# Second mixer of a two-layer hybrid diffusion block: elementwise work moved off GpSimd, small matrix products cut into array tiles, router logits in column tiles

## The chip, the cores and the metric

One Trainium2 chip, one NeuronCore of it. The metric is the device time of one execution in microseconds (us), the median of three runs. The engines are TensorE (PE; its weight loads are listed apart as PEld), VectorE (DVE), ScalarE (ACT), GpSimd (POOL) and SyncE (SP), which issues most DMAs. PE, DVE, ACT and POOL each work through their own instructions in order.

## The reference, cut to what matters

Two layers follow each other on 512 latent and 256 context tokens of width 1024. Each layer is a mixer and then a mixture of 16 experts in which every expert chooses its tokens. Only the second layer's mixer is touched by the change, with the router of both layers.

```
# second mixer: a recurrence in both directions (8 heads of 64), and attention in a window
p = p + mu * (0.5 * (p[t-1] + p[t+1]) - p)                      # centred shift of the projections
w = -softplus(-(w0[d] + tanh(wl) @ w2[d])) - 0.5;  a = sigmoid(a0[d] + al @ a2[d])      # d = 0, 1
dec, keys = exp(-exp(w)), k * (1 + (a - 1) * k_a);  kk = normalised(k * k_k)
S = S * dec + (S @ -kk) (x) (kk * a) + v (x) keys;  y = S @ r    # per token, per direction
win = softmax([scores in a window of 128 | scores on the context | sink]) @ values
# router
aff = softmax(h @ w_router)           # 16 experts; each takes its 64 (context: 32) best tokens
```

## The kernel before, in words

All products are in float32 (two PE passes, so a product counts as two instructions in the trace) except those written as `F32R` or `H16`. A tile framework orders the instructions of the mixers by priority from the program order and inserts the waits; the order on an engine is fixed at build time.

`mixer0`, then `moe` for layer 0, then `mixer1`, then `moe` for layer 1. Within `mixer1`:

- **Front** (`front`, `shifted`, `features`). 33 blocks of 128 columns of the input projection are made by `project` (products `pj`, weights split into two parts by `weights`: `wraw` to `wblk`). `shifted` adds the neighbours in time: ScalarE copies the product to `pd`, GpSimd adds two shifted views into `sh`, and VectorE combines. `features` makes decay, rate and keys for two 128-token tiles of one pair of heads: the low-rank products `lw` with `w2` and `a2`, which are padded with zeros so that each direction uses the whole array, then a chain of elementwise work in the tiles called `lo` (`sig` and `aa`), a scan (`cl`) and the factors A and B, stored in DRAM (`fa`, `fb`).
- **prep**, 24 times (two directions, two groups of heads, six tiles of 128 tokens; two of the six are context tiles). It loads A and B as AR and BK, makes the 64x64 Gram products `gr` of both chunks, masks them (GA, GR), and inverts the triangular matrix by doubling (tiles Th, X, Z, Q; products `pf`, `px`, `pz`, `pc`), with one correction step in float32 (`pe`, tiles Tt and X32).
- **chain**, 24 times two chunks: the recurrence over chunks, with products `an`, `pu`, `pn` and the states `N`; latent tiles also give the output `y`.
- **win_attend**, after the front: 32 head-and-block steps with scores `sw`, softmax weights P (`Pw`), transposes `ptw` to `PTw`, values `po`, and a transpose `orw` of the result to `winT`.
- **finish** and **projected**: group norm of the recurrence's output and the output projection (`op`).

Front, prep, chain and window are generators stepped in turn, so their instructions interleave on every engine. When the last tile's recurrence is done, SBUF is freed for a ring of six 2 MB slots (`open_ring(6)`), two more slots follow when the router's memory is free, and SP then streams 302 MB of expert weights (`we`, `wd`) for layer 1 through them. `route_tile` normalises a tile, transposes it to `ht` and forms the logits `lg`; in layer 0 its stages are stepped between the halves of the output projection (`op`, L774).

The Gram products, and the products of a 64-row state, use zeros in the tile of A to keep two heads apart:

```
for h in range(2):
    for p in range(2):
        nc.sync.dma_start(AR[hd[h], p, :, h], self.fa[d, tt, hd[h], 2 * u + p])   # other half of AR stays zero
...
nc.tensor.matmul(pb[:, 2 * w * c:2 * w * c + 2 * w], BK[:, p, c], AR[:, p, c, :, 0:w // 64], start=True, stop=True)
```

Of the kernel before, what the change touches and what calls it, by code (L numbers as in the profile page):

```python
# [99 lines left out]
class Kern:  # L100
# [690 lines left out]
    def mixer1(self):  # L791
# [69 lines left out]
        def weights():  # L861

            while len(cut) < 2 and (queue or order):
# [8 lines left out]
                (nc.vector if len(order) % 2 else nc.gpsimd).tensor_tensor(w[:, 1], raw, w[:, 0].bitcast(F32), OP.subtract)  # L872
# [9 lines left out]
        nc.gpsimd.tensor_copy(id16[:, 0:128], self.ident)  # L882
        nc.gpsimd.tensor_copy(id16[:, 128:192], id64)
# [46 lines left out]
        def shifted(blk, a, out):  # L930

            n = a[0].shape[2]
            for pb in project(a, 1024 // n):
                yield
            pd = fo.tile([128, NLAT + 2], F32, name="pd")
            nc.gpsimd.memset(pd[:, 0:n + 2:n + 1], 0.0)
            nc.scalar.activation(pd[:, 1:n + 1], pb, AF.Copy)
            s = fo.tile([128, NLAT], F32, name="sh")
            nc.gpsimd.tensor_tensor(s[:, :n], pd[:, 0:n], pd[:, 2:n + 2], OP.add)
            if n < NLAT or blk % 2:  # L940
                nc.vector.tensor_scalar(out, pb, om[:, blk:blk + 1], None, OP.mult)
            else:
                nc.scalar.activation(out, pb, AF.Copy, scale=om[:, blk:blk + 1])
            nc.vector.scalar_tensor_tensor(out, s[:, :n], hm[:, blk:blk + 1], out, OP.mult, OP.add)
# [6 lines left out]
        def features(p, t0, kp, rp, vp, low):  # L951
# [61 lines left out]
            for d in dirs:  # L1013
                nc.gpsimd.tensor_tensor(aa[d], aa[d], kp, OP.mult)
# [164 lines left out]
        def win_attend(ww, kd, V, q, band):  # L1179
# [4 lines left out]
            Ps, PTs, os, sums = {}, {}, {}, {}  # L1184
# [5 lines left out]
            def scores(n):  # L1190
# [23 lines left out]
                nc.vector.reciprocal(m[:, 2:3], m[:, 2:3])  # L1214

            def turn(n):
# [3 lines left out]
                pt = PTs[n] = ww.tile([128, nk, 128], F32, name="PTw", tag="PTw", bufs=3)  # L1220
# [8 lines left out]
            def values(n):  # L1229
                i, b, a = heads[n]  # L1230
                j0, nk = keys(b)
                pt = PTs.pop(n)
# [5 lines left out]
                if a == 0:  # L1238
                    os[n // 2] = ww.tile([128, 128], F32, name="ow", tag="ow", bufs=2)
                nc.scalar.activation(os[n // 2][:, 64 * a:64 * a + 64], po[:, 0:64], AF.Copy, scale=sums.pop(n)[:, 2:3])  # L1240

            def rows(m):
                i, b, _ = heads[2 * m]
                pr = self.bank("orw")
# [907 lines left out]
```

## Time and profile before

| | us |
|---|---|
| three runs | 2968.59, 2965.43, 2972.07 (median 2968.59) |
| the profiled execution: its time | 2972.21 |
| its span, first to last instruction | 2970.4 |
| mean granted TensorE clock | 0.954 of full speed |
| busy: PE, DVE, ACT, POOL | 2660.2, 1322.9, 742.6, 471.4 |

The span divides into layer 0's mixer (to about 560 us), layer 0's experts (to about 1446), the second mixer (1446 to 2205) and layer 1's experts (from 2258, with the first weights from 2204 on). A granted clock of 1.00 is 2.4 GHz, 0.50 is 1.2 GHz; a mean between them over a stretch is a mix of the two. Busy shares hide stages with different limits, so the stages are read one by one.

### The profile page before, as it was taken

The numbers are of one execution on the slowest core, as the hardware profiler recorded it, in microseconds if no ns is written. First come the engines' busy times: TensorE is split into PE (matmuls) and PEld (weight loads), VectorE is DVE, ScalarE is ACT, GpSimd is POOL, SyncE is SP. The second block draws the span as 40 slices with busy tenths as digits, with TensorE's granted clock in tenths as the row PEclk, the third lists the DMA queues.
The fourth block names the chain that finished last, engine by engine and source line by source line (L and its number), as shares of the span: only waits on it lengthen the run. The fifth ranks groups of instructions, "written<-read, shape, count | busy, mean of one in ns | idle before, by whom it ended". The sixth has DMA issues, their size and how long they took to land.

```text
span 2970.4 us, 47837 instructions
## 1 busy us (share of the span) xinstructions
PE 2660.2 (90%) x19606; PEld 1535.4 (52%) x19606; DVE 1322.9 (45%) x3546; ACT 742.6 (25%) x1718; POOL 471.4 (16%) x591
## 2 busy tenths in 40 slices
PE   7999999799999999999878878799987987888886
PEld 4787776544444444444466656587653332333322
DVE  4323665444234334322475777677654332223312
ACT  3212444211111111101354544366321111101111
POOL 2332003200000000000283553411210000000000
PEclk9999999799999999999987988899987999999999
DMA  9765001488988988988642233310349999999997
GB/s 329 244 246 175 27 12 57 172 333 353 371 356 355 371 345 367 365 355 355 216 126 73 86 108 120 111 32 28 118 184 377 426 427 427 427 426 427 426 427 314
DMA packets 176587, 779.47 MB, mean 262 GB/s; under 512 B 24327, under 2 KB 110768, under 8 KB 133488
## 3 DMA queue, kind: packets, MB, share of 16 engines
q1 hardware_dynamic: 169200, 752.31, 64.5%
q0 software_dynamic: 3872, 12.52, 1.2%
q10 hardware_dynamic: 3296, 11.58, 1.0%
q8 instruction: 155, 2.54, 0.4%
q14 instruction: 64, 0.52, 0.1%
HBM read 745.68 MB, written 30.67 MB: 261 GB/s over the span
## 4 chain that ended last, share of the span: by engine, by line
PE 64%; DMA 19%; DVE 9%; POOL 3%; ACT 3%; issue 2%; SPq 0%; POOLq 0%; ACTq 0%; DVEq 0%
PE gu L1924 13%; PE ydn L1992 9%; DMA wd<-in_moe_w_down_dram 8%; DMA we<-in_moe_w_gate_up_dram 8%; PE guc L1937 6%; PE ydc L1996 3%; PE pj L926 3%; PE pj L411 2%; PE pj L412 2%; PE pj L413 2%; PE op L774 2%; PE op L1556 2%; PE adap L231 2%; PE sc L593 1%; PE scp L1816 1%
## 5 line engine op out<-in xcount | busy, mean ns | idle before, releaser
L1924 PE MATMUL gu<-we,xs 128*64 128x512 f32 x3072 | 687.9, 597 | 83.5 <-DMA we<-in_moe_w_gate_up_dram 83.4
L1924 PEld LDWEIGHTS gu<-we,xs 128*64 128x64 f32 x3072 | 216.7, 137 | 520.5 <-issue 408.5
L1992 PE MATMUL ydn<-wd,uT 128*64 128x512 f32 x1536 | 351.8, 600 | 14.3 <-DMA wd<-in_moe_w_down_dram 13.7
L1930 DVE TENSOR_TENSOR sg<-gu,sg 64x512 f32<-64x512 f32 x96 | 66.5, 693 | 458.4 <-ACT sg L1929 457.8
L1929 ACT ACTIVATE sg<-gu 64x512 f32<-64x512 f32 x96 | 56.8, 592 | 846.3 <-PE gu L1924 846.3
L1776 POOL DMA_INDIRECT xg<-xnd,idx x22 | 20.9, 952 | 1246.6 <-DVE gate L1781 1186.0
L1992 PEld LDWEIGHTS ydn<-wd,uT 128*64 128x64 f32 x1536 | 107.9, 137 | 205.3 <-issue 187.0
L1937 PE MATMUL guc<-we,xs 128*32 128x256 f32 x3072 | 172.6, 380 | 0.0
L926 PE MATMUL pj<-aL,wblk 128*128 128x512 f32 x504 | 158.1, 448 | 0.0
L1937 PEld LDWEIGHTS guc<-we,xs 128*32 128x32 f32 x3072 | 96.4, 110 | 68.4 <-issue 7.5
L411 PE MATMUL pj<-ah,wblk 128*128 128x384 f32 (+1 forms) x320 | 109.5, 343 | 1.4 <-ACT ah L380 1.4
L926 PEld LDWEIGHTS pj<-aL,wblk 128*128 128x128 f32 x504 | 99.0, 210 | 18.4
L412 PE MATMUL pj<-al,wblk 128*128 128x384 f32 (+1 forms) x320 | 107.9, 338 | 0.0
L413 PE MATMUL pj<-ah,wblk 128*128 128x384 f32 (+1 forms) x320 | 107.4, 336 | 0.0
L1819 DVE TENSOR_TENSOR x<-scp,x 128x512 f32<-128x512 f32 x144 | 92.3, 684 | 30.3 <-PE scp L1817 29.4
L1996 PE MATMUL ydc<-wd,uTc 128*32 128x256 f32 x1536 | 90.6, 380 | 1.4 <-DMA wd<-in_moe_w_down_dram 1.4
L1906 DVE COPY uTc<-utc 128x128 f32<-128x128 f32 x48 | 14.0, 291 | 172.6 <-PE utc L1904 172.1
L2046 DVE TENSOR_TENSOR yp<-ydn,gbc 64x512 f32<-64x512 f32 x64 | 44.1, 689 | 103.8 <-PE ydn L1992 103.3
L1796 DVE TENSOR_SCALAR xs<-xst,gm,modT 128x128 f32<-128x128 f32 (+1 forms) x88 | 34.8, 397 | 118.9 <-PE xst L1788 115.7
L1900 ACT ACTIVATE uT<-utp 128x256 f32<-128x256 f32 x96 | 36.0, 375 | 159.4 <-PE utp L1899 158.6
L1382 DVE STREAM_TRANSPOSE Zbd<-X 64x256 f16<-64x256 f16 x144 | 62.7, 436 | 24.2 <-ACT X L1376 21.8
L1996 PEld LDWEIGHTS ydc<-wd,uTc 128*32 128x32 f32 x1536 | 47.6, 110 | 43.9 <-issue 15.2
(421 smaller groups left out, 4630.4 us busy)
## 6 DMA issues: line engine op xcount, KB each, us to landing
we<-in_moe_w_gate_up_dram SPq DMA_DIRECT2D x192, 2048.0 KB, 13.5
wd<-in_moe_w_down_dram SPq DMA_DIRECT2D x95, 2048.0 KB, 11.8
adaw<-in_ada_w_dram SPq DMA_DIRECT2D x48, 1024.0 KB, 6.5
wraw<-in_od_w_in_dram SPq DMA_DIRECT2D x33, 512.0 KB, 4.2
wraw<-in_ev_w_in_dram SPq DMA_DIRECT2D x19, 512.0 KB, 6.8
fb<-B SPq DMA_DIRECT2D x24, 256.0 KB, 2.5
BK<-fb SPq DMA_DIRECT2D x24, 256.0 KB, 3.0
xnd<-xn ACTq DMA_DIRECT2D x10, 512.0 KB, 4.7
```

The lines of the kernel that those rows point to most:

```text
L231: nc.tensor.matmul(pb[32 * j:32 * j + 32], self.spad[:, k, :], w[:, 512 * j:512 * j + 512], start=k == 0, stop=k == 7, tile_position=(0, 3 ...
L411: nc.tensor.matmul(pb[:m, :384], w[:, 0, k, 0:m], ah[k][:, t], start=k == 0, stop=False)
L412: nc.tensor.matmul(pb[:m, :384], w[:, 0, k, 0:m], al[k][:, t], start=False, stop=False)
L413: nc.tensor.matmul(pb[:m, :384], w[:, 1, k, 0:m], ah[k][:, t], start=False, stop=k == 7)
L926: nc.tensor.matmul(pb[:, :n], w[:, i, k], a[j][:, k], start=k + i + j == 0, stop=k == 7 and i == 1)
L1382: nc.vector.transpose(Zd[h], X[hd[h]])
L1819: nc.vector.tensor_tensor(xs, pb, xs, OP.add)
L1924: nc.tensor.matmul(gu[64 * j:64 * j + 64, :], g.xs[:, k, 64 * a:64 * a + 64], ws[j][k], start=k == 0, stop=k == 7, tile_position=(0, 64 * j))
L1930: nc.vector.tensor_tensor(sg, gu[64:128], sg, OP.mult)
L1937: nc.tensor.matmul(guc[32 * j:32 * j + 32, 0:256], q.xs[:, k, 32 * a4:32 * a4 + 32], ws[j // 2][k][:, 256 * (j % 2):256 * (j % 2) + 256], ...
L1992: nc.tensor.matmul(y[64 * h:64 * h + 64, :], uT[:, f], wt[i][:, 512 * h:512 * h + 512], start=f == 0, stop=f == 11, tile_position=(0, 64 * h))
L1996: nc.tensor.matmul(yc[32 * j:32 * j + 32, 0:256], uTc[:, f], wt[i][:, 256 * j:256 * j + 256], start=f == 0, stop=f == 11, tile_position=(0 ...
```

## The change

- **GpSimd's work.** The second half of the weight split goes to VectorE always. `shifted` has no copy, no neighbour sum on GpSimd: ScalarE scales the product out of PSUM, and VectorE adds the two neighbours straight from PSUM with two shifted instructions. In `features` three elementwise steps go to ScalarE (`sig`, the scaling of `aa`) and VectorE (`aa` times `kp`). In `prep`, Tt becomes a ScalarE copy (the identity that was subtracted comes back as a product with minus the identity), the masking of Z goes to VectorE, and Zc is copied from PSUM by ScalarE. In `chain` the decay is applied after the sum, by VectorE, and the product `n0s` is gone.
- **Tiles of the array.** `w2` and `a2` hold both directions without zeros and their products use 64 rows each; AR has half the size, no zeros, and is loaded by one DMA (two for context tiles) in the place of four; `gr`, `an` and the first product of `y` use 64-row tiles. `pe` is three kinds of products into one accumulation: the identity once over 256 columns, minus the identity times X over 256 columns, and Tt times X for the four chunks.
- **Window.** ScalarE scales P by the reciprocal sum before the transposes; `values` handles two heads at once, with V as the stationary operand and 128 columns of `PTw` moving, so the transpose `orw` and the per-head copies are gone. `values` comes one step later; `Pw` and `PTw` have four buffers for three.
- **Router.** The logits are formed as four partial sums in column tiles of 32, copied by ScalarE to `ls`, and summed by one product with `rsum`. The router's weights `wr` live in the router's own pool and are loaded when it opens.

```diff
-                (nc.vector if len(order) % 2 else nc.gpsimd).tensor_tensor(w[:, 1], raw, w[:, 0].bitcast(F32), OP.subtract)
+                nc.vector.tensor_tensor(w[:, 1], raw, w[:, 0].bitcast(F32), OP.subtract)
...
-            pd = fo.tile([128, NLAT + 2], F32, name="pd")
-            nc.gpsimd.memset(pd[:, 0:n + 2:n + 1], 0.0)
-            nc.scalar.activation(pd[:, 1:n + 1], pb, AF.Copy)
-            s = fo.tile([128, NLAT], F32, name="sh")
-            nc.gpsimd.tensor_tensor(s[:, :n], pd[:, 0:n], pd[:, 2:n + 2], OP.add)
...
-            nc.vector.scalar_tensor_tensor(out, s[:, :n], hm[:, blk:blk + 1], out, OP.mult, OP.add)
+            nc.scalar.activation(out, pb, AF.Copy, scale=om[:, blk:blk + 1])
+
+            for o, s in ((1, 0), (0, 1)):
+                o = out[:, o:n - 1 + o]
+                nc.vector.scalar_tensor_tensor(o, pb[:, s:n - 1 + s], hm[:, blk:blk + 1], o, OP.mult, OP.add)
...
-                    nc.tensor.matmul(pb[d][:, 0:256], wt[:, d, 128 * p:128 * p + 128], src, start=True, stop=True)
+                    nc.tensor.matmul(pb[d][:, 0:256], wt[64 * d:64 * d + 64, 128 * p:128 * p + 128],
+                                     src[64 * d:64 * d + 64], start=True, stop=True, tile_position=(64 * d, 0))
...
-                        nc.gpsimd.tensor_scalar(sig[d], sig[d], 0.5, 0.5, OP.mult, OP.add)
+                        nc.scalar.activation(sig[d], sig[d], AF.Identity, bias=half, scale=0.5)
...
-                nc.gpsimd.tensor_scalar(aa[d], aa[d], hka[:, p:p + 1], oka[:, p:p + 1], OP.mult, OP.add)
+                nc.scalar.activation(aa[d], aa[d], AF.Identity, bias=oka[:, p:p + 1], scale=hka[:, p:p + 1])
...
-                nc.gpsimd.tensor_tensor(aa[d], aa[d], kp, OP.mult)
+                nc.vector.tensor_tensor(aa[d], aa[d], kp, OP.mult)
...
+                nc.scalar.activation(P, P, AF.Copy, scale=m[:, 2:3])
...
-                    nc.tensor.matmul(po[:, 0:64], pt[:, c], V[:, c if c < 2 else j0 + c, 64 * kv:64 * kv + 64],
-                                     start=c == 0, stop=c == nk - 1)
...
+                    for a in range(2):
+                        nc.tensor.matmul(po[64 * a:64 * a + 64, 0:128],
+                                         V[:, c if c < 2 else j0 + c, 64 * kv:64 * kv + 64], pt[a][:, c],
+                                         start=c == 0, stop=c == nk - 1, tile_position=(0, 64 * a))
...
-                nc.tensor.transpose(pr[:, 0:128], os.pop(m), self.ident)
...
+            for g in range(4):
+                for h in range(2):
+                    nc.tensor.matmul(pb[h][:, w * g:w * g + w], BK[hd[h], g // 2, g % 2],
+                                     AR[hd[h], g // 2, g % 2, 0:w // 64], start=True, stop=True,
+                                     tile_position=(64 * h, 0))
...
-                nc.gpsimd.tensor_tensor(Ttd[h], GA[0:64, :, h], id64[0:64, None, :].to_broadcast([64, 4, 64]),
-                                        OP.subtract)
+                nc.scalar.activation(Ttd[h], GA[0:64, :, h], AF.Copy)
...
-                nc.gpsimd.tensor_tensor(Zd[h], Thd[h], lev(0, 1 - d)[hd[h]], OP.mult)
+                nc.vector.tensor_tensor(Zd[h], Thd[h], lev(0, 1 - d)[hd[h]], OP.mult)
...
+            nc.tensor.matmul(v3(pf), id16[:, 0:128], id16[:, None, 128:192].to_broadcast([128, 4, 64]), start=True,
+                             stop=False)
+            nc.tensor.matmul(v3(pf), minus, X, start=False, stop=False)
             for c in range(4):
-                o = pf[:, 64 * c:64 * c + 64]
-                nc.tensor.matmul(o, Tt[:, c], X[:, c], start=True, stop=False)
-                nc.tensor.matmul(o, id16[:, 0:128], id16[:, 128:192], start=False, stop=True)
+                nc.tensor.matmul(pf[:, 64 * c:64 * c + 64], Tt[:, c], X[:, c], start=False, stop=c == 3)
...
-                nc.gpsimd.tensor_tensor(n0s, n0, dec[:, :, None].to_broadcast([128, 2, 64]), OP.mult)
...
-                        nc.tensor.matmul(pa[hd[h], 64 * p:64 * p + 64], AR[:, p, c, h, 0], n0[:, p],
-                                         start=True, stop=True, tile_position=(0, 64 * h))
+                        nc.tensor.matmul(pa[hd[h], 64 * p:64 * p + 64], AR[hd[h], p, c, 0], n0[hd[h], p],
+                                         start=True, stop=True, tile_position=(64 * h, 64 * h))
...
-                for p in range(2):
-                    nc.vector.scalar_tensor_tensor(N1[:, p], a2_(pn)[:, p], dec[:, p:p + 1], n0s[:, p], OP.mult, OP.add)
+                nc.vector.tensor_tensor(N1, a2_(pn), n0, OP.add)
+                nc.vector.tensor_tensor(N1, N1, dec[:, :, None].to_broadcast([128, 2, 64]), OP.mult)
...
+        for i in range(2):
+            for j in range(4):
+                nc.tensor.matmul(lp[32 * j:32 * j + 32, 0:128], self.rwr[:, 4 * i + j], ht[:, 4 * i + j], start=i == 0,
+                                 stop=i == 1, tile_position=(0, 32 * j))
+        ls = self.rtw.tile([128, 128], F32, name="ls")
+        nc.scalar.activation(ls, lp[:, 0:128], AF.Copy)
...
-        for k in range(8):
-            nc.tensor.matmul(lg[:, 0:16], ht[:, k], self.rwr[:, k], start=k == 0, stop=k == 7)
+        nc.tensor.matmul(lg[:, 0:16], ls, self.rsum, start=True, stop=True)
```

On GpSimd, in the front while the first latent feature blocks are made, these rows stand before (`sh`, `pd`: neighbour sum; `lo`: decay and rate; `Ttbd`, `Zbd`: two tiles of prep; `n0s`: decayed state; `ssq`, `nrm`: norm of the key):

```order
L1428 TENSOR_TENSOR n0s<-N_13101,PL 128x128
L1341 TENSOR_TENSOR Ttbd_12035<-GA,m_11064 64x4x64 x2
L1357 TENSOR_TENSOR Zbd_12031<-Thbd_12029,lev_11053 64x4x64 x2
L939 TENSOR_TENSOR sh<-pd 128x512
L1009 TENSOR_SCALAR lo<-lo,hka,oka 128x256
L936 MEMSET pd 128x2
L1014 TENSOR_TENSOR lo<-lo,ko 128x256
L1009 TENSOR_SCALAR lo<-lo,hka,oka 128x256
L1014 TENSOR_TENSOR lo<-lo,ko 128x256
```

and in the changed kernel GpSimd has, in the whole of that stage, only these kinds:

```order
L1131 TENSOR_SCALAR sgl<-sgl 128x512
L1019 COPY PL<-Pi 128x4 x2
L986 TENSOR_TENSOR ssq<-ssq,mhalf 128x4
L988 COPY nrm<-ssq 128x256
L1019 COPY PL<-Pi 128x4 x2
```

The key's norm and the chunk decays PL stay on GpSimd; everything between them has moved to other engines.

On VectorE, at a prep in the same stage, before (GA, GR: masked Gram products; `Thbd`: Th):

```order
L1331 TENSOR_TENSOR GA<-gr,m_11064 128x256
L1331 TENSOR_TENSOR GR<-gr,m_11064 128x256
L1338 TENSOR_TENSOR Thbd_12040<-GA,m_11064 64x4x64 x2
L1356 STREAM_TRANSPOSE X<-Thbd_12040 64x256 x2
L1435 TENSOR_TENSOR RH<-an,GV 128x128
L1358 TENSOR_TENSOR X<-X,lev_11053 128x256
```

and in the changed kernel:

```order
L1326 TENSOR_TENSOR GA<-gr,m_11093 128x4x64
L1326 TENSOR_TENSOR GR<-gr,m_11093 128x4x64
L1333 TENSOR_TENSOR Thbd_12018<-GA,m_11093 64x4x64 x2
L1350 STREAM_TRANSPOSE X<-Thbd_12018 64x256
L1351 TENSOR_TENSOR Zbd_12020<-Thbd_12018,lev_11082 64x4x64
L1350 STREAM_TRANSPOSE X<-Thbd_12018 64x256
L1351 TENSOR_TENSOR Zbd_12020<-Thbd_12018,lev_11082 64x4x64
L1352 TENSOR_TENSOR X<-X,lev_11082 128x256
```

The two maskings of Z now stand between the transposes, ahead of the X that the next product waits for.

On TensorE, in the window stage, the correction step of a prep stands so before (`gv` is the product of values, `sw` scores; the row of four repeats):

```order
L1398 MATMUL pe<-X_17055,Ttbd_16179 128x64
L1399 LDWEIGHTS id_11063
L1399 MATMUL pe<-id_11063 128x64
L1406 MATMUL gv<-UV,GA 64x64 x8
L1200 MATMUL sw<-kd_16194,qw_16209 128x128
```

and in the changed kernel so:

```order
L1390 LDWEIGHTS id_11092
L1390 MATMUL pe<-id_11092 128x256
L1401 MATMUL gv<-UV,GA 64x64 x8
L1392 MATMUL pe<-X_17770,minus 128x256
L1394 MATMUL pe<-X_17770,Ttbd_12035 128x64 x4
L1199 MATMUL sw<-kd_16082,qw_16096 128x256 x2
```

The identity and `gv` have moved ahead of the products that need X.

## Rows read from the trace of the kernel before

**Rows 1.** Chain of waits, 2300 to 2970: shares by line.
```profile
by line: DMA wd<-in_moe_w_down_dram 36.1%; DMA we<-in_moe_w_gate_up_dram 31.9%; PE ydn L1992 14.0%; PE gu L1924 9.4%; PE scp L1816 2.1%; PE scp L1817 1.8%; PE utp L1899 1.1%; DVE fin L2087 0.8%; PE sel L1771 0.7%; issue 0.3%; POOL rs L281 0
```

**Rows 2.** Engines by stretch: length, busy of PE, PEld, DVE, ACT, POOL, clock, DMA share, GB/s.
```profile
1446.00:1910.00 464.00, 372.72 (x2871) 290.05 (x2868) 320.95 (x682) 214.01 (x501) 238.74 (x329) 0.86 0.35 104
1550.00:1600.00 50.00, 36.82 (x254) 28.80 (x253) 26.30 (x50) 17.90 (x38) 17.77 (x23) 0.69 0.26 71
1910.00:2085.00 175.00, 157.75 (x1753) 134.87 (x1753) 121.52 (x376) 106.10 (x318) 36.33 (x57) 0.94 0.18 54
2085.00:2205.00 120.00, 104.42 (x1097) 68.33 (x1096) 76.89 (x177) 35.44 (x98) 25.92 (x33) 0.90 0.32 110
2258.00:2960.00 702.00, 600.79 (x2812) 224.88 (x2808) 201.11 (x587) 80.07 (x160) 9.15 (x11) 0.99 0.99 417
```

**Rows 3.** Chain of waits, 1446 to 1910 (464 us): shares by line.
```profile
by line: PE pj L926 16.8%; issue 6.2%; PE pe L1398 3.1%; DVE Thbd L1338 2.8%; POOL wblk L872 2.7%; POOL lo L1009 2.5%; POOL lo L1014 2.1%; DVE Zbd L1382 2.1%; POOL ssq L987 2.0%; DVE cl L996 1.9%; PE lw L969 1.9%; DVE X L1356 1.6%; DMA BK<-
```

**Rows 4.** Chain of waits, 1910 to 2085 (175 us): shares by line.
```profile
by line: PE sw L1200 13.6%; PE po L1236 12.0%; PE ptw L1224 6.6%; DVE Thbd L1338 5.4%; PE pe L1398 4.2%; DVE Zbd L1382 3.8%; ACT Pw L1211 3.2%; DVE X L1356 3.1%; DMA Vw<-wvd 3.0%; PE y L1464 2.4%; PE pf L1285 2.4%; PE px L1285 2.4%; issue 2
```

**Rows 5.** Chain of waits, 485 to 560: start us, us, what (one of four alike places).
```profile
505.97 1.69 PE lg L1688 x16
507.66 5.55 PE op L774 x24
```

**Rows 6.** GpSimd by line, 1446 to 2205: busy us, mean ns, idle before, releaser.
```profile
L872 POOL TENSOR_TENSOR wblk<-wraw,wblk 128x1024 fp32r<-128x1024 f32 x17 | 42.0, 2470 | 14.4 <-ACT wblk L871 14.2
L1009 POOL TENSOR_SCALAR lo<-lo,hka,oka 128x256 f32<-128x256 f32 x24 | 22.4, 937 | 3.0 <-DVE t L1008 3.0
L1014 POOL TENSOR_TENSOR lo<-lo,ko 128x256 f32<-128x256 f32 x24 | 18.2, 772 | 0.6
```

**Rows 7.** VectorE and ScalarE by line, 1446 to 2205.
```profile
L872 DVE TENSOR_TENSOR wblk<-wraw,wblk 128x1024 fp32r<-128x1024 f32 x16 | 20.9, 1307 | 2.5 <-ACT wblk L871 2.3
L1338 DVE TENSOR_TENSOR Thbd<-GA,m 64x256 f16<-64x256 f32 x48 | 35.9, 747 | 0.9
L1331 DVE TENSOR_TENSOR GA<-gr,m 128x256 f32<-128x256 f32 x48 | 19.9, 418 | 7.0 <-PE gr L1326 6.4
L1211 ACT ACTIVATE Pw<-sw,wm 128x512 f32<-128x512 f32 (+1 forms) x32 | 23.6, 738 | 25.1 <-DMA UV<-fv 12.8 <-DVE wm L1209 11.5 <-DVE wm L1214 0.7
L1240 ACT ACTIVATE ow<-po,wm 128x64 f32<-128x64 f32 x32 | 10.1, 315 | 9.5 <-PE po L1236 9.2
L1010 ACT ACTIVATE lo<-lo 128x256 f32<-128x256 f32 x24 | 9.8, 410 | 0.0
```

**Rows 8.** TensorE in order of time, clock 1.00: start us, us, line, product.
```profile
1743.56 1.89 PE L969 MATMUL lw<-tl,w 128*128 128x256 f32 x8
...
1976.25 1.00 PE L1236 MATMUL po<-Vw,PTw 128*128 128x64 f32 x8
1977.18 0.45 PE L1448 MATMUL pn<-UV,KBt 128*64 128x64 f32 x8
1977.46 0.40 PE L1432 MATMUL an<-N,AR 128*64 128x64 f32 x8
...
1977.93 1.97 PE L1326 MATMUL gr<-AR,BK 128*128 128x256 f32 x8
1979.74 0.38 PE L1200 MATMUL sw<-kd,qw 128*128 128x128 f32 x2
...
1982.02 0.45 PE L1432 MATMUL an<-N,AR 128*64 128x64 f32 x8
1982.40 0.45 PE L1440 MATMUL pu<-RH,Zf 64*64 64x64 f32 x8
...
2002.04 0.33 PE L1398 MATMUL pe<-X,Ttbd 128*128 128x64 f32 x2
...
2003.17 0.68 PE L1406 MATMUL gv<-UV,GA 64*64 64x64 f32 x16
```

**Rows 9.** TensorE by line and shape, 1000 to 1440 (layer 0's experts, two column tiles).
```profile
L1924 PE MATMUL gu<-we,xs 128*64 128x512 f32 x768 | 168.0, 593 | 0.0
```

More of the change, by code (lines that the diff above doesn't have):

```diff
@@ L882, in mixer1 @@
         nc.gpsimd.tensor_copy(id16[:, 0:128], self.ident)
+        minus = cpl.tile([128, 128], F32, name="minus")
+        nc.scalar.activation(minus, self.ident, AF.Copy, scale=-1.0)
+        half = cpl.tile([128, 1], F32, name="half")
+        nc.gpsimd.memset(half, 0.5)
         nc.gpsimd.tensor_copy(id16[:, 128:192], id64)
@@ L1183, in win_attend @@
             heads = [(i, b, a) for i in range(4) for b in range(4) for a in range(2)]
-            Ps, PTs, os, sums = {}, {}, {}, {}
+            Ps, PTs = {}, {}
             def keys(b):
@@ L1229, in values @@
             def values(n):
-                i, b, a = heads[n]
+                i, b, _ = heads[n]
                 j0, nk = keys(b)
-                pt = PTs.pop(n)
+                pt = [PTs.pop(n + a) for a in range(2)]
                 kv = i // 2
@@ L1235, in values @@
                 for c in range(nk):
-                    nc.tensor.matmul(po[:, 0:64], pt[:, c], V[:, c if c < 2 else j0 + c, 64 * kv:64 * kv + 64],
-                                     start=c == 0, stop=c == nk - 1)
[L1238 to L1244, printed above, removed]
-                nc.tensor.transpose(pr[:, 0:128], os.pop(m), self.ident)
-                nc.scalar.activation(late["winT"][:, i, 128 * b:128 * b + 128], pr[:, 0:128], AF.Copy)
+                    for a in range(2):
+                        nc.tensor.matmul(po[64 * a:64 * a + 64, 0:128],
+                                         V[:, c if c < 2 else j0 + c, 64 * kv:64 * kv + 64], pt[a][:, c],
+                                         start=c == 0, stop=c == nk - 1, tile_position=(0, 64 * a))
+                nc.scalar.activation(late["winT"][:, i, 128 * b:128 * b + 128], po[:, 0:128], AF.Copy)
             for n in range(len(heads) + 4):
@@ L1252, in win_attend @@
                     turn(n - 2)
-                if 3 <= n < len(heads) + 3:
-                    values(n - 3)
-                if n >= 5 and n % 2:
-                    rows((n - 5) // 2)
+                if n >= 4 and n % 2 == 0:
+                    values(n - 4)
                 yield
@@ L1304, in prep @@
             ps_ = slice(2 * u, 2 * u + 2)
[L1305 removed]
+            cr = st_.pool
+            AR = cr.tile([128, 2, 2, 2, 64], F32, name="AR")
             BK = new([128, 2, 2, 128], "BK")
[L1307 removed]
+            if lat:
+                nc.sync.dma_start(AR, self.fa[d, tt, :, ps_])
+            else:
                 for p in range(2):
[L1309 to L1312 removed]
+                    nc.sync.dma_start(AR[:, p, :, 0], self.fa[d, tt, :, 2 * u + p, :, 0])
             nc.sync.dma_start(BK, self.fb[d, tt, :, ps_].rearrange("q p c k s -> q p c (k s)"))
@@ L1450, in chain @@
                 N1 = rf.tile([128, 2, 64], F32, name="N1", tag=f"N{d}{u}", bufs=3)
-                for p in range(2):
-                    nc.vector.scalar_tensor_tensor(N1[:, p], a2_(pn)[:, p], dec[:, p:p + 1], n0s[:, p], OP.mult, OP.add)
+                nc.vector.tensor_tensor(N1, a2_(pn), n0, OP.add)
+                nc.vector.tensor_tensor(N1, N1, dec[:, :, None].to_broadcast([128, 2, 64]), OP.mult)
                 N0[d, u] = N1
```

68 lines of the change are left out of this document (30 added, 38 removed).

## The prediction

> **What bounds the kernel now.** I read the chain of waits from the end backwards first, because the largest part of the span lies there. From 2300 on it consists of DMAs of expert weights and the products that wait for them [rows 1], and the table of stretches shows the DMA engines 0.99 busy at 417 GB/s over 702 us [rows 2]. The change touches nothing there, so that stage keeps its length and starts when the ring opens, at the end of the second mixer. Each microsecond that the mixer gives back moves the end by one; each that the change saves behind the opening is worth nothing.
>
> The same table shows three different stretches of the mixer [rows 2]. In the front (A, 464 us) TensorE is busy for 372.7 us, 0.80 of it, VectorE 0.69, ScalarE 0.46, GpSimd 0.51, and the granted clock is 0.86. In the window (B, 175 us) TensorE is busy 0.90, VectorE 0.69, ScalarE 0.61, GpSimd 0.21. In the tail (C, 120 us) it is 0.87, 0.64, 0.30 and 0.22. So in B and C a product taken from TensorE is worth nearly its time; in A no engine is full, and the chain must say what ends last. There TensorE's products `pj` hold 16.8%, and behind them stands a long row of steps on all engines, three of them on GpSimd: `wblk` 2.7%, `lo` L1009 2.5% and L1014 2.1% of 464 us, that is 12.5, 11.6 and 9.7 us [rows 3]. In B the chain is TensorE's: `sw` 13.6%, `po` 12.0% (21 us), `ptw` 6.6% [rows 4].
>
> **The change part by part.** The sum is made against the profiled execution, 2972.2 us; its end stands 3.6 us above the median of the three runs.
>
> *Router.* In layer 0 the chain passes four times through `lg`, 16 instructions in 1.69 us, ahead of the next `op` [rows 5]. They become 16 instructions of 128 columns on four column tiles and a sum over two. Column tiles do overlap in this kernel: 768 instructions `gu` of 512 columns on two of them took 168.0 us, 0.219 us each [rows 9], while `sw` and `gr` of 256 columns take 1.81/8 = 0.226 us on the whole array [rows 8]. A 128-column instruction is half of that, 0.11 us. With four at a time 16 take 0.45 us, with two 0.9, without overlap 1.8, and the sum some 0.2. I take 0.9: 4 x (1.69 - 0.9) = -3 us, between -4 and +1. The copy to `ls` waits a stage later behind `op`, 5.55 us long, which hides it. `wr` is loaded later and through GpSimd's own queue; if it came late, the first logits would wait, at most a few us. In layer 1 one such group gives -1.
>
> *A, off TensorE.* The second half of the weight split takes 2.47 us on GpSimd and 1.31 on VectorE [rows 6, 7]: of 12.5 us on the chain 47% go, -5.9. The scaling L1009 takes 0.94 us on GpSimd; a ScalarE instruction of its shape takes 0.41: 56% of 11.6, -6.5. The product L1014 takes 0.77 and on VectorE 0.42 to 0.75 (L1331 and L1338, the nearest shapes): -4.4 to -0.3, taken as -2. `Thbd` L1338 is 2.8% of the chain, 13.0 us; it takes 747 ns, though it has half the partitions of L1331 with 418 ns. The row of A shows GpSimd at work for half of the stage. If it slows VectorE's work on SBUF, most of that goes with GpSimd's work: 44% of 13.0 is -5.7; if it does not, 0. I take -5.7, since the same number of elements per partition stands in both rows. For `sh`, Z and the decayed state, each under the smallest share shown (1.6%, 7.4 us), I take -3, between 0 and -7. Together -23.
>
> *A, on TensorE.* `lw` took 1.89 us for 8 instructions of 256 columns [rows 8]; with 64 rows, two at a time, 0.95. It is 1.9% of the chain, 8.8 us: -4. `gr` has 8 of 256 columns in 1.81 us and becomes 16 of 128 in pairs, 0.9; it is below the shares shown, -3 (0 to -7). No product here pairs long row tiles, so both bounds stay: without overlap these are +2 instead of -7. `pe` took 1.13 us for four steps [rows 8], first `pe` to first `gv`. Now it has one 256-column pass for the identity (0.11, ahead of the wait for X), two of 256 columns for minus X (0.45) and eight of 64. Eight of `po`, with a weight load for each, took 0.93 us, which is 0.12 each; by columns alone they would take 0.03 x 8 x 2 = 0.45. So 1.0 to 1.5 us, +0.2 for each of some 15 preps: +3, between -2 and +6.
>
> *Changes of tiling.* Eight `pn` ahead of `an`, both on 64-column tiles, pass in 0.28 us; eight `an` ahead of `pu`, on another tiling, in 0.38 [rows 8]. So a change costs about 0.1 us. Counted over the two programs' order on TensorE, changes outside the experts rise from 304 to 491. All on the path they would be +19 us. In A I put 3 us for them (some 100 changes, a third of them on the chain), in B 5. The Trainium skill, TensorEngine Tiling (Array Packing), Key Properties, states that changing the tiling mode drains TensorE; the 0.28 and 0.38 agree, and by that rule on every change the sum below would be -29 in the place of -40. The same list says that tiles load and multiply independently, for which `gu` is the only long row here.
>
> A is thus -23 - 4 - 3 + 3 + 3 = -24, between -45 and -5.
>
> *B.* `po` is 8 instructions of 64 columns in 0.93 us [rows 8], 0.116 each. There are 288 before and after, now of 128 columns in two column tiles, 0.055 each by the overlap of `gu`. The chain has 21 us of it, so -11; without overlap -1. The transpose `orw` and `gr` are below the 2.4% (4.2 us) that ends the row: -2 each. `Thbd` 5.4% (9.5 us) x 44% is -4. `pe`: +1.4. Tiling +5. ScalarE loses 10.1 us of copies [rows 7] and gains 32 scalings of P, like `Pw` 0.74 us each, 23.6 us, and some 21 copies of Tt and Zc, 0.41 each, 8.6 us: 106.1 becomes 128, of 163. Since each scaling stands between the softmax and the transposes I charge 1; `values` a step later and the fourth buffers of P cover the rest. If they do not, 32 x 0.74 = +24. B: -12, between -28 and +8.
>
> *C* has its chain in the output projection and the norms; fewer columns in `gr` stand against longer `pe`: 0, between -5 and +5.
>
> The sum is -3 - 24 - 12 + 0 - 1 = -40: 2932 profiled, **2928** as a median.
>
> **The rivals.**
> *VectorE or ScalarE becomes the bound.* In A VectorE has 321 us and gets 17 splits (+22), 15 second neighbour sums of up to 512 columns (0.75 each, +11), some 30 maskings of Z and 24 products (0.42 to 0.75 each, +23 to +40), less 10 for `Thbd`: 367 to 384 of 440 us, 0.83 to 0.87, as full as TensorE in C. Queued behind them stand X and GA, for which TensorE waits. Then A gives half, -12, and with ScalarE in the same place B gives nothing: 2940 to 2952. For it speaks the in-order queue, against it the shorter `Thbd`.
> *The tiles don't overlap.* Then `lw`, `gr` and `po` give -1 + 2 in the place of -20: 2949. `gu` speaks against it for columns; for rows nothing does.
> *The clock rises in A.* At 1.00 in the place of 0.86 the 358 us that TensorE still has there shrink by 50; with half of it on the path, 2903, with all, 2878. For it: fewer waits between products.
> *Nothing is gained.* Every shortened wait in A uncovers another as late: 2963 to 2974.
> *Slower: the clock falls in A.* TensorE keeps less work among the same waits on loads and scans. The stretch from 1550 to 1600, busy 0.74, has a clock of 0.69 [rows 2]. If all of A went there, its 358 us at 0.86 would become 446: +88, 3016. It decides from 358 x 0.86/c = 398 on, a clock of 0.77. Against it: the waits shrink with the work. The Trainium skill, TensorE: Matmul & The Clock Gate, Part 1, says that the clock follows how busy the array has been, and thus speaks for this case; the two rows of A agree in direction.
>
> **How the numbers follow.** The sum and what lies near it, 2905 to 2937: 0.48. VectorE or ScalarE in the way: 0.19. Clock up: 0.14. No overlap: 0.06. Nothing: 0.05. Clock down: 0.08. The likeliest is 2928. The range 2890 to 2960 leaves out the last two and the deeper half of the rise in clock, about 0.2. A difference under 0.2% (6 us) can't be told from none here. All cases up to 2960 are faster, 0.87; nothing is 0.05; clock down is slower, 0.08.
>
> **What would show it.** The profile of the changed kernel should have the ring open some 40 us earlier and the weights' stretch unchanged at 417 GB/s; A near 440 us with a clock of at least 0.86, no GpSimd line but `ssq` on its chain and `Thbd` under 500 ns; B near 163 us with `po` at half its share; `lw` and `gr` at half their time for the same columns. `Thbd` still at 750 ns, `lw` or `gr` unshortened, VectorE busy over 0.87 in A, ScalarE's scaling of P on B's chain, or a clock under 0.8 in A would each show the step that failed. If the gain lies in C or behind the opening, the whole argument is wrong.

## The result and the profile after

The changed kernel took 2928.45 us as a median of four executions (2918.84 to 2939.24) beside 2968.86 for the kernel before on the same chip: a ratio of 0.9865 with a 95% interval of [0.9828, 0.9902]. A second set, timed later beside the kernel before, gave 0.9877 [0.9859, 0.9896]. The eight executions of the changed kernel lie 20 us apart, those of the kernel before beside them 13 (2965.43 to 2978.91).

The stretches of the changed kernel, as the table by stretch gives them (length, busy of PE, PEld, DVE, ACT, POOL, clock, DMA share, GB/s); they answer to A, B, C and the weights' stretch of [rows 2]:

```profile
1444.00:1878.00 434.00, 363.14 (x2977) 278.54 (x2973) 315.45 (x759) 241.98 (x581) 54.22 (x88) 0.88 0.38 112
1878.00:2046.00 168.00, 144.71 (x1773) 114.95 (x1772) 118.70 (x390) 125.92 (x341) 5.84 (x6) 0.93 0.17 49
2046.00:2150.00 104.00, 95.72 (x1062) 60.83 (x1060) 69.27 (x166) 38.11 (x106) 5.84 (x4) 0.98 0.37 129
2212.00:2914.00 702.00, 598.52 (x2810) 223.38 (x2806) 200.08 (x585) 79.02 (x158) 8.92 (x11) 1.00 0.99 417
```

The last row is the same stage at the same 417 GB/s: it only starts earlier. GpSimd fell from 238.7 to 54.2 us in A, and VectorE, which took over much of that work, is busy for less than before.

To compare stage by stage I cut both traces at the same instructions: the first `we` of layer 0, the first `wraw` of the second mixer, the first and the last `pj` of a latent block, the last `po`, the last `pn`, the first `gu` of layer 1, the end. Layer 0's experts, 887 to 890 us in all five, are left out. Each column is one profiled execution. The same cuts serve for the experiments.

| us between cuts | before | after | after, second set | GpSimd only | tiles only |
|---|---|---|---|---|---|
| to the first `we` (router of layer 0 in it) | 567.0 | 564.2 | 562.6 | 567.8 | 562.7 |
| context part of A | 90.6 | 82.6 | 83.0 | 81.3 | 92.0 |
| latent part of A | 358.0 | 336.8 | 329.1 | 333.9 | 354.7 |
| B | 191.7 | 184.2 | 185.6 | 191.0 | 184.5 |
| C | 96.2 | 92.4 | 98.3 | 95.2 | 94.7 |
| to the first `gu` | 66.8 | 62.8 | 63.9 | 66.9 | 63.4 |
| layer 1's experts | 712.9 | 714.0 | 714.6 | 714.3 | 713.5 |

Of the 45.8 us between the two profiled spans, 29 came from A, 7.5 from B, 4 each from C and the opening, 3 from the first router.

The chain of waits after, by line, in A and then in B; it answers to [rows 3, 4]:

```profile
by line: PE pj L929 20.9%; issue 7.3%; PE gr L1319 3.0%; DVE wblk L872 2.4%; PE pe L1394 2.3%; DMA wraw<-in_od_w_in_dram 2.2%; POOL ssq L986 2.0%; ACT lo L971 1.9%; DVE X L1350 1.9%; DVE cl L995 1.9%; PE pn L1441 1.8%; DVE Zbd L1376 1.8%; D
by line: PE sw L1199 8.9%; ACT Pw L1210 7.6%; issue 5.7%; ACT Pw L1214 5.6%; PE po L1238 4.3%; DVE Zbd L1376 3.4%; ACT PTw L1226 3.2%; PE pe L1394 3.0%; PE ptw L1224 2.6%; DVE X L1350 2.6%; PE gv L1401 2.5%; ACT UV L1436 2.4%; DVE wm L1207 
```

Of GpSimd only `ssq` is left among the lines shown in A. Added up over the whole chain there, beyond the lines that the row shows, GpSimd's part fell from 73 us to 21 us (`ssq`, `nrm`, `aL` and what lies near them). In B TensorE's three window products fell from 32% to 16%, and ScalarE's two passes over P, 13%, stand in their place.

VectorE by line, 1444 to 2160; the first three rows answer to [rows 6, 7], the others to the two rows of before in the fence behind it:

```profile
L872 DVE TENSOR_TENSOR wblk<-wraw,wblk 128x1024 fp32r<-128x1024 f32 x33 | 40.1, 1219 | 2.1 <-ACT wblk L871 2.0
L1333 DVE TENSOR_TENSOR Thbd<-GA,m 64x256 f16<-64x256 f32 x48 | 19.8, 412 | 0.8
L1013 DVE TENSOR_TENSOR lo<-lo,ko 128x256 f32<-128x256 f32 x24 | 10.3, 440 | 0.9 <-ACT lo L1008 0.6
L1020 DVE TENSOR_TENSOR A<-kk,lo 128x256 f32<-128x256 f32 x24 | 10.0, 418 | 0.9 <-DMA fa<-A 0.8
L1030 DVE TENSOR_TENSOR B<-lo,cl 128x256 f32<-128x256 f32 x24 | 10.0, 418 | 0.0
```

```profile
L1021 DVE TENSOR_TENSOR A<-kk,lo 128x256 f32<-128x256 f32 x24 | 17.5, 727 | 3.1 <-DMA fa<-A 2.9
L1031 DVE TENSOR_TENSOR B<-lo,cl 128x256 f32<-128x256 f32 x24 | 14.5, 605 | 2.3 <-POOL lo L1014 2.2
```

`Thbd`, L1013 and the lines of A and B now take 0.41 to 0.44 us. Why three of them took longer is seen in the order of time of the kernel before (start, us, engine, line):

```profile
1581.74 2.39 POOL L872 TENSOR_TENSOR wblk<-wraw,wblk 128x1024 fp32r<-128x1024 f32 x1
1582.01 2.67 DVE L944 SCALAR_TENSOR_TENSOR al<-sh,hm,al 128x512 f32<-128x512 f32 x1
...
1618.78 1.29 DVE L1338 TENSOR_TENSOR Thbd<-GA,m 64x256 f16<-64x256 f32 x2
1618.83 1.84 POOL L1341 TENSOR_TENSOR Ttbd<-GA,m 64x256 f32<-64x256 f32 x2 [1.11 <-DVE GA L1331]
```

The VectorE operation that starts at 1582.01 ends at 1584.68, 0.55 us behind the end of GpSimd's at 1584.13. Most others of this shape on its line take 0.73 to 0.75 us, so most of it ran after GpSimd's operation and not beside it. Of the two `Thbd` the first, begun before GpSimd, is short and the second twice as long. So it is in the whole kernel before: of the 40 `Thbd` that began behind a two-operand operation of GpSimd still at work, 39 ended 0.28 us behind its end.

TensorE after, in order of time:

```profile
1779.49 1.13 PE L967 MATMUL lw<-tl,w 64*128 64x256 f32 x8
...
1956.91 1.31 PE L1238 MATMUL po<-PTw,Vw 128*64 128x128 f32 x20
1958.15 0.45 PE L1433 MATMUL pu<-RH,Zf 64*64 64x64 f32 x8
...
1959.25 1.28 PE L1319 MATMUL gr<-AR,BK 64*128 64x128 f32 x16
1960.51 0.77 PE L1224 MATMUL ptw<-ks,Pw 128*128 128x128 f32 x5
```

These answer to [rows 8]: 8 `lw` in 1.13 in the place of 1.89, 16 `gr` in 1.26 in the place of 8 in 1.81, and 20 `po` in 1.24, 0.062 each, for 0.116. Row tiles overlap too, though `lw` and `gr` came to 0.60 and 0.70 of their time and not to the half of a full overlap. The router's group, [rows 5], became on the chain

```profile
533.31 0.77 PE lgp L1691 x16
534.08 5.66 PE op L774 x24
```

### The profile page after: what moved, and what is told of

Read it like the earlier page. It is cut to its first block, busy times and chain, and to the rows that moved or that the text cites. A ratio compares the mean times of both kernels' runs of the same rounds, so it can differ in the third digit from the quotient of the medians.

```text
span 2924.6 us, 47862 instructions
## 1 busy us (share of the span) xinstructions
PE 2625.6 (90%) x19778; PEld 1484.6 (51%) x19778; DVE 1316.1 (45%) x3649; ACT 796.1 (27%) x1841; POOL 243.1 (8%) x278
## 4 chain that ended last, share of the span: by engine, by line
PE 65%; DMA 18%; DVE 9%; ACT 4%; issue 2%; POOL 1%; SPq 0%; POOLq 0%; ACTq 0%; DVEq 0%
PE gu L1934 14%; PE ydn L2002 9%; DMA wd<-in_moe_w_down_dram 9%; DMA we<-in_moe_w_gate_up_dram 7%; PE guc L1947 6%; PE pj L929 3%; PE ydc L2006 3%; PE pj L411 2%; PE pj L412 2%; PE pj L413 2%; PE op L774 2%; PE op L1550 2%; PE adap L231 2%; PE sc L593 1%; PE scp L1826 1%
## 5 line engine op out<-in xcount | busy, mean ns | idle before, releaser
L2006 PE MATMUL ydc<-wd,uTc 128*32 128x256 f32 x1536 | 90.6, 381 | 1.6 <-DMA wd<-in_moe_w_down_dram 1.6
L1803 ACT ACTIVATE xs<-xst,modT,gm 128x128 f32<-128x128 f32 (+1 forms) x88 | 38.3, 448 | 118.7 <-DVE xs L1806 117.7
```

Of the source, the lines that this page charges most:

```text
L2006: nc.tensor.matmul(yc[32 * j:32 * j + 32, 0:256], uTc[:, f], wt[i][:, 256 * j:256 * j + 256], start=f == 0, stop=f == 11, tile_position=(0 ...
```

## The experiments

Each was timed in rounds beside the kernel before on its chip.

| kernel | median | before | ratio, 95% interval |
|---|---|---|---|
| changed kernel again | 2935.87 | 2972.40 | 0.9877 [0.9859, 0.9896] |
| GpSimd's work only | 2940.73 | 2972.40 | 0.9885 [0.9865, 0.9905] |
| tiles only | 2960.75 | 2972.40 | 0.9964 [0.9950, 0.9977] |
| old window | 2940.53 | 2972.40 | 0.9896 [0.9877, 0.9915] |
| scratch work, two operands | 2955.41 | 2969.00 | 0.9944 [0.9927, 0.9961] |
| scratch work, one operand | 2941.80 | 2969.00 | 0.9904 [0.9888, 0.9921] |
| P scaled on GpSimd | 2944.79 | 2969.00 | 0.9912 [0.9889, 0.9936] |
| P scaled on VectorE | 2937.92 | 2969.00 | 0.9890 [0.9872, 0.9909] |
| prep's GpSimd work only | 2960.71 | 2972.06 | 0.9965 [0.9955, 0.9975] |
| front's GpSimd work only | 2952.11 | 2972.06 | 0.9934 [0.9911, 0.9957] |
| X before GR and Z | 2935.34 | 2972.06 | 0.9884 [0.9865, 0.9903] |
| old form of `pe` | 2942.41 | 2972.21 | 0.9897 [0.9880, 0.9913] |

My theory was that GpSimd's part gives most of the gain, through VectorE's and the chain's waits; the rivals were that TensorE's tiles give it, and that only GpSimd's own latency counted.

**The changed kernel again.**

> The changed kernel once more, beside the three that follow, to have it on the same chip and to see how far its own executions lie apart: 2918 to 2939 us were seen, so a median of 2923 to 2934 is expected by every theory.

Its median is a little above the expectation, its ratio the same. All else was set beside both sets.

**The two parts.** One kernel has the hunks of the change on `wblk`, `shifted`, `features`, Tt with `pe`, Z, Zc and the state alone, the other all the rest alone. Of the first, on the kernel before:

```diff
+                nc.vector.tensor_tensor(w[:, 1], raw, w[:, 0].bitcast(F32), OP.subtract)
...
+                nc.scalar.activation(Ttd[h], GA[0:64, :, h], AF.Copy)
```

and of the second:

```diff
+                    nc.tensor.matmul(pb[d][:, 0:256], wt[64 * d:64 * d + 64, 128 * p:128 * p + 128],
+                                     src[64 * d:64 * d + 64], start=True, stop=True, tile_position=(64 * d, 0))
...
+                nc.scalar.activation(P, P, AF.Copy, scale=m[:, 2:3])
```

> Only GpSimd's work is moved (weight split, neighbour sum, the steps on lo, Tt with the new form of pe, Z, Zc, the decayed state); all products stay on the whole array as before, window and router too. Theory: the front's gain is the waits on and beside GpSimd, so this alone gives some 23 us in A and 4 in B, less 4 for the longer pe: 2946, between 2938 and 2955. Rival, the gain is TensorE's: 2960 to 2972, since the work only moves to engines that are then fuller.

> Only the tiles: lw, gr, an, y, the window's values with V stationary, and the router; GpSimd's work is as before. Theory: router 4, lw and gr 7 to 9, po and orw 13, less 8 for changes of tiling: about 16 us, 2953, between 2945 and 2961. Rival, the gain is TensorE's: 2930 to 2942. If the two parts simply add, the gains of this run and of the one with GpSimd's work alone sum to the changed kernel's 40.

GpSimd's part gave 1.15%, 34 us, the tiles 0.36%, 11 us; together 45, and the whole change gave 37 to 40, which the intervals allow. By the table of cuts, GpSimd's part shortened A by 33 us (9 and 24) and little else; the tiles took 4 from the router, 2 from A, 7 from B, 3 from the opening. The theory held, and its size for A was too small; the tiles gave 11 us where 16 were expected.

**Where in A.** The two halves of GpSimd's part, each on the kernel before. Prep's half is Tt with `pe`, Z, Zc and the decayed state, the front's `wblk`, `shifted` and the three steps on `lo`:

```diff
+                nc.vector.tensor_tensor(Zd[h], Thd[h], lev(0, 1 - d)[hd[h]], OP.mult)
...
+            nc.scalar.activation(Zc, v3(pz), AF.Copy)
```

```diff
+                nc.vector.tensor_tensor(w[:, 1], raw, w[:, 0].bitcast(F32), OP.subtract)
...
+                nc.vector.tensor_tensor(aa[d], aa[d], kp, OP.mult)
```

> The kernel before with only prep's and the chain's work taken from GpSimd (Tt with the new form of pe, Z, Zc, the decayed state); weight split, neighbour sum and the steps on lo stay on GpSimd, all tiles are the old ones. From the run with scratch work, where just such operations beside Th cost some 22 us: 22 less 4 for the longer pe is 18, so 2949 to 2955 where the kernel before takes 2970. By the sum of the prediction (Th 10, the share for Z and the state 2, less 4 for pe): 2960 to 2964.

> The other half: the kernel before with only the weight split, the neighbour sum and the three steps on lo taken from GpSimd. By the sum of the prediction 5.9 + 6.5 + 2 + 1 us: 2952 to 2958. If VectorE's waits beside GpSimd's two-operand work in prep were all of the gain, nothing: 2967 to 2973. Both halves together should give the 32 us of the run with all of GpSimd's work moved.

They gave 10 us and 20 us, at or a little above the sums of the prediction (6 to 10, and 15) and not what the run with scratch work, told of below, had made me expect. They add up to 30 us, where the two together gave 34. With prep's part alone `Thbd` is short, 428 ns, but GpSimd's remaining work meets VectorE elsewhere (the row of A in the kernel with prep's part, then that of `Thbd` in the one with the front's):

```profile
L1025 DVE TENSOR_TENSOR A<-kk,lo 128x256 f32<-128x256 f32 x24 | 21.0, 873 | 3.6 <-DMA fa<-A 3.1 <-ACT lo L1014 0.4
```

```profile
L1335 DVE TENSOR_TENSOR Thbd<-GA,m 64x256 f16<-64x256 f32 x48 | 36.6, 763 | 0.9
```

**Contention or latency.** The changed kernel with GpSimd work whose results nobody uses:

```diff
+                nc.gpsimd.tensor_tensor(jk[:, h], GA[0:64, :, h], id64[0:64, None, :].to_broadcast([64, 4, 64]), OP.subtract)
...
+                nc.gpsimd.tensor_tensor(jz[hd[h]], Thd[h], lev(0, 1 - d)[hd[h]], OP.mult)
```

and, in the second kernel, each line twice as a scaling with one operand:

```diff
+                nc.gpsimd.tensor_scalar(jk[:, h], GA[0:64, :, h], 0.5, 0.5, OP.mult, OP.add)
```

> The changed kernel, and on GpSimd again the four operations of each prep that went away (GA minus identity, Th times its level mask), but into scratch tiles that nobody reads: 96 operations of two operands from SBUF, some 70 us of GpSimd's time, on no chain. Theory: what was lost on VectorE was lost beside GpSimd's two-operand work, so Th goes back from 412 towards 750 ns, and the time grows by 6 to 14 us: 2937 to 2948 where the changed kernel is at 2928 to 2936. Rival, only GpSimd's own place on the chain counted: Th stays at 412 ns and the time within 3 us.

> The same scratch work in the form of scalings with one operand, twice as many of them (192). If it is the second operand from SBUF that makes VectorE wait, Th stays near 412 ns and the time within 3 us of the changed kernel's. If any work of GpSimd on SBUF slows VectorE, Th grows and the time is that of the run with two operands, 6 to 14 us more.

The first lost 20 to 23 us against the two sets of the changed kernel (0.9944 less 0.9877 or 0.9865, times 2969). That is more than the 6 to 14 us forecast, in the direction forecast. So work on no chain took back more than half of the gain. `Thbd` and the scratch operation beside it, and `Thbd` in the second kernel:

```profile
L1335 DVE TENSOR_TENSOR Thbd<-GA,m 64x256 f16<-64x256 f32 x48 | 31.5, 657 | 0.7
L1339 POOL TENSOR_TENSOR jk<-GA,m 64x256 f32<-64x256 f32 x48 | 35.8, 761 | 280.5 <-DVE GA L1326 280.0
```

```profile
L1335 DVE TENSOR_TENSOR Thbd<-GA,m 64x256 f16<-64x256 f32 x48 | 23.2, 484 | 0.8
```

With one operand, 86 us of GpSimd's time for 72, the scratch work still cost 8 to 12 us: less than with two, but more than the 3 expected. The intervals of the ratios overlap here, though each of its six executions (2938 to 2948 us) lies above the four of the changed kernel's second set (2928 to 2937). The expectation of "near 412 ns" failed too, at 484. So latency as the only cause is out; that one-operand work is harmless is out as well.

Another rival would be that the scratch work holds the tiles GA and Th that it reads, so that others wait for them. The waits of the first kernel leave little room for it. The first line is the only wait for the scratch work that the profile shows, 3.4 us once, and no scratch operation stands on the chain; the second is TensorE's wait for X, 22.9 us in the changed kernel:

```profile
PEld L1278 <- POOL jz L1355: 3.4, 1, 3.4
PE pf L1278 <- DVE X L1356: 31.0, 15, 3.5
```

One-operand work does not let VectorE pass either. In the second kernel, in order of time:

```profile
1722.24 0.56 POOL L1339 TENSOR_SCALAR jk<-GA 64x256 f32<-64x256 f32 x1
1722.46 0.60 DVE L1335 TENSOR_TENSOR Thbd<-GA,m 64x256 f16<-64x256 f32 x1
```

`Thbd` ends 0.27 us behind the scaling. So did 34 of the 46 that began beside a running scaling, and the other 12, beside scalings about to end, took their 0.41 us; with two-operand work all 28 that began beside it ended 0.28 us behind it. What differs is the length of GpSimd's operation: 0.43 to 0.49 us on average for a scaling, 0.76 for the others.

The latent part of A (between the cuts) tells how VectorE's lost time becomes the kernel's. The rows are, in this order, of the kernel before, the changed kernel, the changed kernel in its second set, and the kernel with two-operand scratch work:

```profile
1544.80:1902.80 358.00, 296.61 (x2399) 226.67 (x2398) 240.51 (x529) 155.35 (x380) 165.65 (x226) 0.86 0.30 91
```

```profile
1534.50:1871.30 336.80, 290.58 (x2491) 219.11 (x2492) 237.78 (x591) 176.58 (x440) 25.85 (x45) 0.88 0.33 99
```

```profile
1534.90:1864.00 329.10, 282.20 (x2491) 211.45 (x2492) 237.83 (x591) 177.09 (x440) 26.14 (x46) 0.91 0.34 101
```

```profile
1538.00:1894.20 356.20, 300.38 (x2491) 225.67 (x2490) 249.34 (x591) 177.13 (x440) 65.85 (x97) 0.84 0.31 93
```

TensorE's busy time times the clock is 255, 256, 257 and 252 us: its work did not shrink. What changed is its idle time, 61, 46, 47 and 56 us, and the clock, a mean of the two levels 1.2 and 2.4 GHz, 0.86, 0.88, 0.91 and 0.84. Of the 21 us that the change gained here, 15 are idle time and 6 busy time at a higher clock; in the second set the same idle time came with 14. With the 11.5 us more that VectorE was busy beside the scratch work came 9 to 10 us of idle time and 10 to 18 of products at a lower clock.

**Does TensorE's work count in A?** The old form of `pe`, with Tt less the identity made by VectorE behind X:

```diff
-                nc.scalar.activation(Ttd[h], GA[0:64, :, h], AF.Copy)
...
+                nc.vector.tensor_tensor(Ttd[h], GA[0:64, :, h], id64[0:64, None, :].to_broadcast([64, 4, 64]), OP.subtract)
```

> The changed kernel with the old form of pe, and Tt made as GA minus the identity by VectorE, behind X (48 operations of some 0.4 us more on VectorE, 48 copies of 0.41 us less on ScalarE). The new form occupies TensorE for 22.8 us in the front where the old one took 19.0, and in the window 11.5 for 8.4. If TensorE's products count, the old form gives 3 to 7 us: 2926 to 2930 against 2933 for the changed kernel. Rival: VectorE's 20 us of work, beside X and GA on its queue, take it back: 2931 to 2940.

The rival held in its direction: 0.9897 for 0.9877 or 0.9865, so some 6 to 10 us slower, at the edge of what the intervals part (its 2942 us lie just above the range; the changed kernel was not timed on that chip). In A VectorE got more and TensorE's products, at full clock, less (289.6 x 0.86 = 249):

```profile
1542.20:1884.00 341.80, 289.61 (x2503) 218.17 (x2504) 247.16 (x617) 167.39 (x414) 26.38 (x45) 0.86 0.33 97
```

Six us less of TensorE's time at full clock did not outweigh 9 us more on VectorE. The edit changes both at once, so it prices neither alone.

**An order that brings X earlier.** `masked` does one kind of masking for both heads:

```diff
+            masked(0, GA)
...
             nc.vector.tensor_tensor(X, X, lev(0), OP.mult)
+            if lat:
+                masked(1, GR)
+            for h in range(2):
+                nc.vector.tensor_tensor(Zd[h], Thd[h], lev(0, 1 - d)[hd[h]], OP.mult)
```

> The changed kernel with another order on VectorE in prep: both GA maskings, Th, both transposes and X first, the masked GR and the two maskings of Z behind them. TensorE's idle time ahead of pf, 22.9 us with X as releaser, is the longest of the products there; X comes 1.3 us earlier in 16 preps and 0.5 us in 8. Theory: a part of that is on the chain, 4 to 12 us faster than the changed kernel (2933 as a median of its eight runs), so 2921 to 2929. Rival, the interleaved work covers it, or the banks of gr, held longer, take it back: 2930 to 2938.

TensorE's idle time ahead of `pf` with X as releaser fell from 22.9 to

```profile
  DVE X L1351: 11.3, 9
```

and the time did not move: 0.9884. In the latent part of A TensorE stayed idle for 47 us, as before that edit, so the wait went elsewhere. B was 191.2 us long in this profile, for 184.2 and 185.6. The rival held.

**The window.** First the old window in the changed kernel (V moving, `orw`, no scaling of P ahead of the transposes):

```diff
+                    nc.tensor.matmul(po[:, 0:64], pt[:, c], V[:, c if c < 2 else j0 + c, 64 * kv:64 * kv + 64],
+                                     start=c == 0, stop=c == nk - 1)
```

then the scaling of P on GpSimd, and in a third kernel on VectorE:

```diff
-                nc.scalar.activation(P, P, AF.Copy, scale=m[:, 2:3])
+                nc.gpsimd.tensor_scalar(P, P, m[:, 2:3], None, OP.mult)
```

> The changed kernel with the old window: per-head values with PTw stationary, the transpose orw, no scaling of P, three buffers, values a step earlier. Theory: the window's part is worth about 9 us net (11 and 2 on TensorE, less 1 for ScalarE and 3 for tiling), so 2937, between 2932 and 2945. Rival, ScalarE's scaling of P eats it: 2925 to 2931, no slower than the changed kernel.

> The changed kernel with the scaling of P on GpSimd in the place of ScalarE (one operand, 32 of 512 and 640 columns). Theory: in B ScalarE's 24.7 us of scaling stand in the chain with 5.6% of 168 us, so B shortens by 3 to 8 us: 2922 to 2930 on a chip where the changed kernel takes 2930 to 2936. Rival, another wait is as late (TensorE is busy 0.86 there): within 3 us.

> The changed kernel with the scaling of P on VectorE. VectorE is busy 118.7 of 168 us in B and gets 32 operations of 0.3 to 0.7 us, 10 to 22 us. Theory, ScalarE's queue is what waits in B: 2 to 6 us faster than the changed kernel. Rival, VectorE's queue is as tight: 0 to 5 us slower.

The old window took 2940.5 for 2935.9 on its chip: 5 us with intervals that overlap, so its worth lies between nothing and the 9 expected; B itself was 188.0 us long for 184.2 and 185.6. Taking the scaling from ScalarE came with a longer B in both cases, one profiled execution each: 193.5 with GpSimd and 197.9 with VectorE. Of the latter's 12 to 14 us more, 8 are TensorE's busy time at a clock of 0.86 for 0.93. The time was no better with either; on GpSimd it was 10 to 14 us worse than the changed kernel by the ratios, which neither of the two expectations had, and on VectorE it lay within the rival's 0 to 5 in the second set. GpSimd takes more than twice ScalarE's 720 ns for it:

```profile
L1214 POOL TENSOR_SCALAR Pw<-Pw,wm 128x512 f32<-128x512 f32 x16 | 25.0, 1563 | 57.3 <-DVE wm L1213 27.9 <-DVE sw L1202 7.7 <-ACT winT L1241 7.2
```

That ScalarE's queue bounds B, as its share of the chain suggests, is not borne out.

No version beat the changed kernel.

## Why the prediction was right, point by point

**The total**, 40 us, is that of the first set; the second gave 37. It rests on two terms that erred against each other, A too small and B too large, and on several that held. That it fits to the microsecond is luck; that the gain lies in A and comes from GpSimd's part is not.

**Router, -3**: 2.8 and 4.4 in the two profiles; 16 partial products took 0.77 us, for 0.9 forecast. **The opening, -1**: 3 to 4. **Layer 1's experts, 0**: 1.1 to 1.7 longer.

**A off TensorE, -23**: shown by the kernel with GpSimd's part alone, and too small; A measured -33 there, with the longer `pe`, forecast at +3, already in it. The step that was mis-sized is the one that priced GpSimd's work by three lines of the chain and `Thbd`. `Thbd` went to 412 ns as assumed, L1014 became 440 ns, at the good end of its bounds, L1009 as a ScalarE operation took 590 ns and not 410. What the sum lacked is that the same collision held up other operations of two operands, for which it has no term: the factors A and B, 727 and 605 ns, became 418. Of GpSimd's 73 us on the chain it also priced 34 by lines and gave -3 for the others that move, in which `sh`, L975 and Z hold 15. How much of the difference each omission makes, no run separates. VectorE is busy for 315 us in A where I expected 367 to 384, and the rival in which it becomes the bound did not come. Shorter A, B and `Thbd` are one reason. That tally was also too high by itself: it left on VectorE the scaling of 17 blocks that ScalarE took over (10 us), and took 0.42 to 0.75 us for a masking of Z that measured 0.25. The Trainium skill, SBUF — State Buffer, SBUF: two separate sides, states that VectorE's operations with two inputs from SBUF and GpSimd's operations that read SBUF exclude each other for a whole instruction; the pair at 1582.01 and the `Thbd` beside scalings agree, and by that rule the sum would have been larger.

**The clock.** I kept it apart as a rival, with 0.14. The rows show some of it inside the forecast case: the granted clock in the latent part was 0.88 and 0.91 where it had been 0.86, worth 6 and 14 us. That the shorter idle time raised it is not shown. The profiled executions of 329 and 337 us there differ by clock, not by idle time, and over all kernels the link is loose: seven profiled executions with 44 to 47 us of idle time there had clocks from 0.85 (the old window) to 0.91, seven with 52 to 62 us had 0.84 to 0.89. The slower rival, a falling clock, did not come; TensorE's busy share of the latent part rose from 0.83 to 0.86.

**A on TensorE, -1**: the tiles alone gave -2, with the old `pe`, where the sum without `pe` has -4. `lw` and `gr` overlap, less than hoped, and at full clock the tiles save 5 us of TensorE's work in the latent part (296.6 x 0.857 before, 292.9 x 0.851 with tiles), where `lw` and `gr` are busy for 6.7 and 4.3 us less. The rest fits the charge for changes of tiling, but no run separates it.

**B, -12**: -6 to -7.5. The terms on TensorE's products were right in sum: `po`, `orw`, `gr` and `pe` have -13.6, and TensorE is busy some 155 us between the cuts for 169. `Thbd`, at -4, gave nothing to be seen: with GpSimd's part alone, `pe` in it, B is 191.0 us long for 191.7. What failed besides is the sentence that in B a product taken from TensorE is worth nearly its time: half of the 14 us became idle time (23 us before, 30 after). The old window and the two places for the scaling fit the view that TensorE, ScalarE and VectorE hold each other there; which wait decides stays open.

**C, 0**: -4 and +2 in the two profiled executions. TensorE is busy for 95% of C, and its work at full clock is 85 to 87 us in all three; the clock was 0.93 before, 0.99 and 0.91 after, and makes the difference.

## What to carry to other kernels

Before pricing a move off GpSimd by its place on the chain, look for VectorE's operations with two inputs from SBUF whose mean is far above others of the same shape: they wait for GpSimd, and that time comes back with the move. Here it paid for the work that VectorE took over: 315 us busy in A for 321. Where TensorE is not full, judge a change by the idle time between its products and not by the columns it saves: in A 5 us of saved products came with a gain of 2, and the whole change came with 15 us less idle time. Read the granted clock of each profile beside it, since 6 and 14 us of the latent part's gain are clock, which differed as much between two executions of one kernel. Where three engines are over 0.7 busy, as in the window after, one of them may give back half of what it saves, as here.

## What was not expected of the hardware

`Thbd`, an operation of two operands on VectorE, took 747 ns on average with GpSimd's beside it and 412 without; another, on 128x512 (0.75 us alone), that met a GpSimd operation of 2.39 us took 2.67. GpSimd's scalings with one operand stop it in the same way: beside 192 of them `Thbd` took 484 ns on average, ending 0.27 us behind a scaling that was running, and the kernel 8 to 12 us more. Two 64-row tiles overlap for products of 128 and 256 columns: 16 `gr` in 1.26 us are 0.079 us each, where a 128-column product on the whole array would take, by an estimate from the 0.226 of 256 columns, 0.113.
